# Where the two operands of a matmul start within a line of 256 bytes: MLP layers and output projection shifted by 128, 192 and 160 bytes

## The chip, the cores and the metric

The kernel runs on one core of one Trainium2 chip. The metric is the device time of one execution in microseconds. The kernel before was timed three times: 1135.06, 1134.04 and 1132.4 us, median 1134.04. A fourth execution was profiled and took 1130.94 us, with a span of 1129.1 us from its first to its last instruction.

## The reference

One layer of a streaming encoder on 512 frames of 1024 channels, all in float32. Three token mixers run on one input projection, their gated sum goes through an output projection, and a squared-ReLU MLP follows:

```
p   = rms_norm(x, g1) @ w_in                       # 1024 -> 11520 columns
m   = gate_a * y_a + gate_b * y_b + gate_c * y_c   # short conv, RG-LRU, RWKV-7
x   = x + m @ w_out                                # 1024 x 1024
h2  = rms_norm(x, g2)
x   = x + square(relu(h2 @ w1)) @ w2               # 1024 -> 4096 -> 1024
out = rms_norm(x, gf)
```

The mixers y_a, y_b and y_c matter here only as the work that runs before and beside the output projection.

## The kernel before

**Three matmuls for one product.** A float32 product is made of three matmuls in a reduced float32 format (`fp32r`). Each operand is split into a high part, a copy into that format, and a low part, the rest. `mm3` (L157 to L160) adds high × high, high × low and low × high in PSUM. In each matmul one operand is stationary: 128 × 128 values are loaded into TensorE by a separate instruction, the weight load ("PEld", LDWEIGHTS). The other is moving: 128 rows by 512 or 256 columns stream through. Every matmul has its own weight load, and the load for the next matmul runs while the present one streams.

**Weights of the network.** `load_half` (L132) fetches a 128 × 512 block on SP's queue, ACT copies it into `whi` (L136), and DVE subtracts to get `wlo` (L138, in the profile the helper's L99). Four buffers of each rotate. All blocks of `w_in`, `w_out`, `w1` and `w2` go this way, 340 half blocks in all.

**The stages that the change touches** come last:

- The output projection `w_out(th)` (L853) runs in two halves of 256 frames. For each of 8 output blocks and 8 input blocks it does one `mm3`: stationary a slice of `whi`/`wlo`, moving the merged `mh`/`ml` of `open_m` (L803). The first half is woven into the last part of the RWKV recurrence, the second runs alone. That is 2 × 8 × 8 × 3 = 384 matmuls of 256 columns, named `acc<-mh,whi` and the like in the profile. The result, scaled and split, is written into `h2h`/`h2l` (L862 to L864).
- The first MLP layer (`mlp1`, L908) does 32 blocks of 8 `mm3`, stationary `whi`/`wlo`, moving `h2h`/`h2l`, 512 columns each; the first block is done in two halves of 256. The squared ReLU is split into `ah`/`al` for the first 24 blocks and `ah2`/`al2` for the last 8 (L930 to L934).
- The second MLP layer (`mlp2`, L952) has the roles turned: stationary a 128-column slice of `ah`/`al` (or `ah2`/`al2`), moving `whi`/`wlo` with 512 columns. It keeps eight PSUM banks open and does 32 × 4 × 2 `mm3`.

**Places in memory.** Each tile has one start address, the same in all 128 partitions. `AL = 256` makes a tile start at a multiple of 256 bytes, `ALM = 2048` at a multiple of 2048. `whi`, `wlo`, `hh`, `hl` (the normalised input of the first projection), `mh`, `ml`, `ah2` and `al2` have AL; `h2h`, `h2l`, `ah` and `al` have ALM. A slice of 128 columns is 512 bytes and a row of 512 columns is 2048, so in all large matmuls before both operands start at 0 within a line of 256 bytes. A few small tiles of the mixers have no such demand. The program's memory plan puts them at other places within a line: `bd`, `bh` and `bl` at 128, `lgh`, `lgl`, `lws` and `las` at 224, `swah` and `swal` at 64, `swch`, `swcl`, `uh` and `ul` at 32. Their matmuls stand among those of the first projection (`pp<-hh,whi`).

The order of instructions is made when the program is built, by a planner with priorities; the change gives it the same instructions with the same shapes.

Of the kernel before, what the change touches and what calls it, by code (L numbers as in the profile page):

```python
# [10 lines left out]
F32R = mybir.dt.float32r  # L11
# [7 lines left out]
P = 128  # L19
# [10 lines left out]
S = 512  # L30

AL, ALM = 256, 2048
D = 1024
KT = 8
# [59 lines left out]
def block_kernel(ctx, tc, xt, win, par, mulr, sw, wout, w1, w2, fg, cst, eyes, out):  # L94
# [28 lines left out]
    x2d = dp.tile([4, P, D], F32, name="x2d")  # L123

    pv = lambda n, j: part[:, PI[n], j:j + 1]


    def load_w(src):
# [497 lines left out]
    def gate_c(pool, q, tag):  # L626
        gt = pool.tile([P, S], F32, tag=tag, name=tag, bufs=2 if tag[0] == "b" else 1)
        t = yield from proj(("gc", q))
        ac.activation(gt, t, AF.Tanh, bias=pv("mgc", q), scale=0.5)
        return gt  # L630

    def g2_mul(pool, q, gt):
        swh, swl = load_sw(pool, "swc", q, 4, 1)
        pg = pm.tile([P, S], F32, tag="pm", name="pg2")
        mm3(pg, swh[:, 0], swl[:, 0], lgh, lgl)
        stt(gt, gt, 1.0, pg, ADD, MUL)
# [13 lines left out]
    M = {"done": []}  # L650
# [112 lines left out]
    def fill_main(g):  # L763
        a = AB[g]
        if g + 1 == NG:
            yield from a
            return
        end = object()
        while not GS[g].inv_done:
            if next(a, end) is end:  # L770
                break
            yield
        while not GS[g].inv_done:
            yield
        b = krv(g + 1, GS[g + 1])
        live = [b, a]
        while live:
            for x_ in list(live):
                if next(x_, end) is end:
                    live.remove(x_)  # L780
                else:
                    yield
# [20 lines left out]
    def open_m():  # L803
        pk_ctx.close()
        mo = mo_ctx.enter_context(tc.tile_pool(name="mo", bufs=1))
        mh = M["mh"] = mo.tile([P, KT, S], F32R, name="mh", align_bytes=AL)
        ml = M["ml"] = mo.tile([P, KT, S], F32R, name="ml", align_bytes=AL)
        mab = M["mab"] = mo.tile([P, 2, S], F32, name="mab")
        for q in M["done"]:
            gp.dma_start(mh[:, q], mhd[q])  # L810
            gp.dma_start(ml[:, q], mld[q])
        gp.dma_start(mab, mpd[6:8].rearrange("q p t -> p q t"))
        M["mo"] = mo
        return
        yield

    def last_fill():
        yield from fill_main(NG - 1)
        M["gts"] = []
        for h in range(2):  # L820
            q = 6 + h
            gt = yield from gate_c(sp, q, f"bv{h}")
            g2_mul(wk, q, gt)
            M["gts"].append(gt)
            yield
        wk_ctx.close()
        ht_ctx.close()
        h2p = h2_ctx.enter_context(tc.tile_pool(name="h2p", bufs=1, side="right"))
        M["h2h"] = h2p.tile([P, KT, S], F32R, name="h2h", align_bytes=ALM)
        M["h2l"] = h2p.tile([P, KT, S], F32R, name="h2l", align_bytes=ALM)  # L830
        xrp = xr_ctx.enter_context(tc.tile_pool(name="xrp", bufs=1, side="right"))
        M["xrp"] = xrp
        x2T = M["x2T"] = xrp.tile([P, KT, S], F32, name="x2T")
        for i in range(4):
            gp.dma_start(x2T[:, 2 * i:2 * i + 2], xt[2 * i:2 * i + 2].rearrange("k p t -> p k t"))
        while "half" not in M:
            yield
        fin_m(0)
        yield from w_out(0)
# [3 lines left out]
    def fin_m(th):  # L843
        tl = slice(th * HT, (th + 1) * HT)
        for h in range(2):
            y = G_.v[h][:, tl]
            tt(y, y, G_.bv[h][:, tl], ADD)
            stt(y, y, 0.5, M["gts"][h][:, tl], MUL, MUL)
            tt(y, y, M["mab"][:, h, tl], ADD)
            ac.copy(M["mh"][:, 6 + h, tl], y)  # L850
            tt(M["ml"][:, 6 + h, tl], y, f(M["mh"][:, 6 + h, tl]), SUB)

    def w_out(th):  # L853
        tl = slice(th * HT, (th + 1) * HT)
        for mo in range(KT):
            w = load_w(wout[mo])
            acc = pp.tile([P, S], F32, tag="pp", name="acc")[:, 0:HT]
            for q in range(KT):
                mm3(acc, *wslice(w, q), M["mh"][:, q, tl], M["ml"][:, q, tl], start=q == 0, stop=q == KT - 1)
            x2 = M["x2T"][:, mo, tl]  # L860
            tt(x2, acc, x2, ADD)
            hi = M["h2h"][:, mo, tl]  # L862
            ac.activation(hi, x2, AF.Copy, scale=pv("n2", mo))
            stt(M["h2l"][:, mo, tl], x2, pv("n2", mo), f(hi), MUL, SUB)  # L864
            yield
# [15 lines left out]
    def post_half(th):  # L881
        yield from post_norm(NG - 1, G_, 4 * th, 4 * th + 4)
        if th == 0:
            M["half"] = True

    fl = last_fill()
    segments([(chainit(amat(G_), inverse(G_), open_m()), R4),
              (chainit(chain(G_, 0, 4), post_half(0), chain(G_, 4, NC), post_half(1)), R5)], fl)
    drain(fl)
# [3 lines left out]
    h2h, h2l = M["h2h"], M["h2l"]  # L893
# [6 lines left out]
    NA = 3 * NF // 4  # L900
    with tc.tile_pool(name="mw", bufs=2) as mw, \
            tc.tile_pool(name="ap", bufs=1) as apool, \
            ExitStack() as apool2:
        ahs = [apool.tile([P, NA, S], F32R, name="ah", align_bytes=ALM)]
        als = [apool.tile([P, NA, S], F32R, name="al", align_bytes=ALM)]
        ahl = lambda fi: (ahs[fi // NA][:, fi % NA], als[fi // NA][:, fi % NA])

        def mlp1(t, w, tl):  # L908
# [5 lines left out]
        for fi in range(NF):  # L914
            t = pp.tile([P, S], F32, tag="pp", name="p1")
# [150 lines left out]
```

## Time and profile before

| What | Value |
|---|---|
| Median of three runs | 1134.04 us |
| Profiled execution, its own time | 1130.94 us |
| Its span | 1129.1 us |
| TensorE busy (PE) | 1090.0 us, 97% |
| Weight loads busy (PEld) | 866.7 us, 77% |
| VectorE (DVE) and ScalarE (ACT) busy | 786.8 and 549.2 us |
| Mean granted TensorE clock | 0.984 |
| Output projection, first and last matmul | 709.0 to 768.7 us |
| First MLP layer, first and last matmul | 768.8 to 945.0 us |

A matmul's busy time runs from its start to its modelled end and overlaps that of the next one, since matmuls are pipelined; what a stream costs is the distance between the starts. Rows of groups show line, engine, operation, output and inputs, the stationary part's size, the moving part's size and type, the count, the busy time in us and the mean of one in ns, then the idle time before them. For three stretches of time the profile also lists each engine's busy time and count, then the granted clock, the share of DMA and its GB/s.

### The profile page before, as it was taken

How to read it: one execution, taken by the hardware profiler on the slowest of the kernel's cores; microseconds unless marked ns; L12 is line 12 of the kernel's file. 1: busy time of each engine (PE TensorE's matmuls, PEld its weight loads, DVE VectorE, ACT ScalarE, POOL GpSimd, SP SyncE). 2: the span in 40 equal slices, each digit the busy share in tenths (PEclk: the TensorE clock that was granted, in tenths of full speed). 3: DMA queues.
4: the chain of work that ended last, by engine and by line, in shares of the span. 5: the costliest groups of instructions: out<-in, count | busy, mean ns of one | idle time of the engine just before them, and what ended most of it. 6: DMA issues, size and time to landing. Idle time of an engine off the chain costs nothing.

```text
span 1129.1 us, 17256 instructions
## 1 busy us (share of the span) xinstructions
PE 1090.0 (97%) x6396; PEld 866.7 (77%) x6396; DVE 786.8 (70%) x1537; ACT 549.2 (49%) x1005; POOL 59.6 (5%) x99
## 2 busy tenths in 40 slices
PE   8899989999989999989999989999999999999996
PEld 4677867678777778777778767899888888888885
DVE  7998996889986989986888967686544544222225
ACT  6655356544466634466644465565444443222224
POOL 3200000000000000000000020100000000000003
PEclk8899988999999999999999999999999999999999
DMA  5222222222233222233222262555323225322232
GB/s 183 80 98 66 84 78 73 65 91 71 89 104 103 67 89 71 89 108 93 66 94 69 75 191 99 170 181 167 100 93 103 94 95 187 101 93 93 97 106 88
DMA packets 61973, 114.69 MB, mean 102 GB/s; under 512 B 7232, under 2 KB 10816, under 8 KB 61888
## 3 DMA queue, kind: packets, MB, share of 16 engines
q1 hardware_dynamic: 54960, 95.49, 25.7%
q0 software_dynamic: 6352, 17.30, 4.8%
q8 instruction: 50, 0.82, 0.3%
q10 hardware_dynamic: 576, 0.79, 0.2%
q14 instruction: 35, 0.29, 0.1%
HBM read 104.64 MB, written 8.91 MB: 101 GB/s over the span
## 4 chain that ended last, share of the span: by engine, by line
PE 82%; DVE 13%; issue 3%; ACT 2%; DMA 0%; SPq 0%; DVEq 0%; ACTq 0%
PE pp L160 12%; PE pp L158 12%; PE pp L159 11%; PE acc L159 6%; PE acc L158 6%; PE acc L160 6%; PE p L160 5%; PE p L159 5%; PE p L158 5%; DVE wlo L99 3%; PE pA L463 2%; DVE Z L99 2%; DVE dg L99 2%; PE py L570 1%; PE pu L555 1%
## 5 line engine op out<-in xcount | busy, mean ns | idle before, releaser
L99 DVE TENSOR_TENSOR wlo<-raw,whi 128x512 fp32r<-128x512 f32 x340 | 235.7, 696 | 231.4 <-ACT whi L136 222.7
L136 ACT CAST whi<-raw 128x512 fp32r<-128x512 f32 x340 | 209.6, 619 | 353.4 <-PE acc L160 123.1
L160 PE MATMUL pp<-hh,wlo 128*128 128x512 f32 x696 | 280.8, 404 | 18.5 <-DVE wlo L99 18.4
L159 PE MATMUL pp<-hl,whi 128*128 128x512 f32 x696 | 277.8, 399 | 3.1 <-DVE hl L102 3.1
L158 PE MATMUL pp<-hh,whi 128*128 128x512 f32 x696 | 278.5, 402 | 1.6 <-ACT hh L259 1.5
L160 PEld LDWEIGHTS pp<-hh,wlo 128*128 128x128 f32 x696 | 132.1, 190 | 55.4 <-DVE wlo L99 27.9
L159 PEld LDWEIGHTS pp<-hl,whi 128*128 128x128 f32 x696 | 132.2, 190 | 31.0 <-DVE hl L102 3.7
L158 PEld LDWEIGHTS pp<-hh,whi 128*128 128x128 f32 x696 | 132.2, 190 | 29.9 <-ACT hh L259 1.9
L160 PE MATMUL p<-h2h,wlo 128*128 128x512 f32 (+1 forms) x264 | 101.2, 383 | 0.0
L158 PE MATMUL p<-h2h,whi 128*128 128x512 f32 (+1 forms) x264 | 101.2, 383 | 0.0
L159 PE MATMUL p<-h2l,whi 128*128 128x512 f32 (+1 forms) x264 | 101.0, 383 | 0.0
L159 PE MATMUL acc<-wlo,ah 128*128 128x512 f32 x256 | 99.7, 389 | 0.0
L158 PE MATMUL acc<-whi,ah 128*128 128x512 f32 x256 | 99.6, 389 | 0.0
L160 PE MATMUL acc<-whi,al 128*128 128x512 f32 x256 | 99.6, 389 | 0.0
L159 PEld LDWEIGHTS p<-h2l,whi 128*128 128x128 f32 x264 | 49.6, 188 | 9.7
L158 PEld LDWEIGHTS p<-h2h,whi 128*128 128x128 f32 x264 | 49.6, 188 | 9.6
L160 PEld LDWEIGHTS p<-h2h,wlo 128*128 128x128 f32 x264 | 49.6, 188 | 9.5
L159 PEld LDWEIGHTS acc<-wlo,ah 128*128 128x128 f32 x256 | 48.0, 188 | 10.1 <-DVE wlo L99 0.3
L158 PEld LDWEIGHTS acc<-whi,ah 128*128 128x128 f32 x256 | 48.0, 188 | 10.1
L160 PEld LDWEIGHTS acc<-whi,al 128*128 128x128 f32 x256 | 48.0, 188 | 10.0
L99 DVE TENSOR_TENSOR Z<-Z,dg 64x31 f32<-64x31 f32 (+15 forms) x124 | 42.2, 340 | 4.1
L99 DVE TENSOR_TENSOR dg<-Z 64x31 f32<-64x31 f32 (+15 forms) x124 | 42.2, 340 | 4.1
(299 smaller groups left out, 1532.3 us busy)
## 6 DMA issues: line engine op xcount, KB each, us to landing
raw<-in_win SPq DMA_DIRECT2D x180, 256.0 KB, 2.6
raw<-in_w SPq DMA_DIRECT2D x128, 256.0 KB, 2.6
raw<-in_wout SPq DMA_DIRECT2D x32, 256.0 KB, 2.6
swr<-in_sw SPq DMA_DIRECT2D x16, 128.0 KB, 2.2
x2T<-in_xt POOLq DMA_DIRECT2D x4, 512.0 KB, 6.2
x2d<-st POOLq DMA_DIRECT2D x8, 256.0 KB, 2.9
xr<-x2d POOLq DMA_DIRECT2D x1, 2048.0 KB, 9.1
xT<-in_xt SPq DMA_DIRECT2D x3, 512.0 KB, 6.4
```

The costliest lines, as they stand in the source:

```text
L99: return v.tensor_tensor(out=o, in0=a, in1=b, op=op)
L136: ac.copy(hi, raw)
L158: pe.matmul(ps, wh, xh, start=start, stop=False)
L159: pe.matmul(ps, wh, xl, start=False, stop=False)
L160: pe.matmul(ps, wl, xh, start=False, stop=stop)
L463: pe.matmul(pts[h][:, ci], G_.BK[rows, jj, c], G_.AR[rows, jj, c], start=True, stop=True)
L555: pin(e != 0, pe.matmul(pu[64 * h:64 * h + 64, jj], AXt[rows, e, c, 0], sv[rows, e], start=True, stop=True))
L570: mm = pe.matmul(py[64 * h:64 * h + 64, jj], w, x, start=first and jj == 0, stop=last, skip_group_check=True)
```

## The change

Six tiles get a new start within the line of 256 bytes. A helper makes a tile that is longer by some bytes, on a multiple of 256, and returns the part behind them, seen as blocks of 512 columns:

```diff
+    def shifted(pool, n, name, by):
+
+        t = pool.tile([P, by // 4 + n * S], F32R, name=name, align_bytes=AL)
+        return t[:, by // 4:].rearrange("p (k t) -> p k t", k=n)
...
-        mh = M["mh"] = mo.tile([P, KT, S], F32R, name="mh", align_bytes=AL)
-        ml = M["ml"] = mo.tile([P, KT, S], F32R, name="ml", align_bytes=AL)
+        mh = M["mh"] = shifted(mo, KT, "mh", 160)
+        ml = M["ml"] = shifted(mo, KT, "ml", 160)
...
-        M["h2h"] = h2p.tile([P, KT, S], F32R, name="h2h", align_bytes=ALM)
-        M["h2l"] = h2p.tile([P, KT, S], F32R, name="h2l", align_bytes=ALM)
+        M["h2h"] = shifted(h2p, KT, "h2h", 128)
+        M["h2l"] = shifted(h2p, KT, "h2l", 128)
...
-        ahs = [apool.tile([P, NA, S], F32R, name="ah", align_bytes=ALM)]
-        als = [apool.tile([P, NA, S], F32R, name="al", align_bytes=ALM)]
+        ahs = [shifted(apool, NA, "ah", 64)]
+        als = [shifted(apool, NA, "al", 64)]
```

`whi` and `wlo` stay at 0. Counted from the stationary to the moving operand, the difference is 160 in the output projection and 128 in the first layer, where the shifted tile moves, and 0 - 64 = 192 modulo 256 in the second layer, where it is stationary. `ah2`, `al2` and the first projection's `hh`, `hl` keep their places. The start of the six tiles changes from a multiple of 2048 (of 256 for `mh` and `ml`) to one of 256 plus the shift.

## The prediction

> **What bounds the kernel now.** I read the page first, for the engine that sets the end and for the stretches in which it has no gap.
>
> ```profile
> span 1129.1 us, 17256 instructions
> PE 1090.0 (97%) x6396; PEld 866.7 (77%) x6396; DVE 786.8 (70%) x1537; ACT 549.2 (49%) x1005; POOL 59.6 (5%) x99
> PEclk8899988999999999999999999999999999999999
> PE 82%; DVE 13%; issue 3%; ACT 2%; DMA 0%; SPq 0%; DVEq 0%; ACTq 0%
> ```
>
> TensorE is busy for 97% of the span and carries 82% of the chain that ended last. Next the busy time in three stretches: the first MLP layer, the second, and the output projection.
>
> ```profile
> 773.70:944.70 171.00, 171.00 (x768) 141.75 (x767) 86.70 (x132) 76.20 (x133) 2.17 (x4) 1.00 0.31 103
> 945.30:1105.00 159.70, 159.70 (x706) 132.26 (x705) 41.86 (x61) 37.80 (x61) 1.29 (x2) 1.00 0.33 112
> 709.00:773.50 64.50, 63.66 (x600) 59.81 (x599) 50.57 (x119) 38.49 (x86) 5.11 (x8) 1.00 0.55 180
> ```
>
> In both layers PE has no idle time at the full clock, and DVE and ACT are busy for about half of the time or less. In the projection PE is idle for 0.84 of 64.5 us. So here the time is the number of matmuls times the distance from one start to the next, and a nanosecond on each moves the end by as much. The groups of the whole run count them:
>
> ```profile
> L158 PE MATMUL p<-h2h,whi 128*128 128x512 f32 x248 | 96.7, 390 | 0.0
> L158 PE MATMUL p<-h2h,whi 128*128 128x256 f32 x16 | 4.5, 283 | 0.0
> L158 PE MATMUL acc<-whi,ah 128*128 128x512 f32 x256 | 99.6, 389 | 0.0
> L159 PE MATMUL acc<-ml,whi 128*128 128x256 f32 x128 | 37.0, 291 | 0.0
> ```
>
> Each product has three such groups: 744 matmuls of 512 columns and 48 of 256 in the first layer, 768 of 512 in the second, 384 of 256 in the projection. The timeline of TensorE gives the distance. Its columns are start and duration in us; between the two rows of a pair lie 196, then 136 steps.
>
> ```profile
> 799.73 0.39 PE L158 MATMUL p<-h2h,whi 128*128 128x512 f32 x1
> ...
> 844.15 0.39 PE L159 MATMUL p<-h2l,whi 128*128 128x512 f32 x1
> ...
> 752.27 0.28 PE L158 MATMUL acc<-mh,whi 128*128 128x256 f32 x1
> ...
> 768.59 0.28 PE L159 MATMUL acc<-ml,whi 128*128 128x256 f32 x1
> ```
>
> 44.42 us / 196 = 226.6 ns and 16.32 us / 136 = 120.0 ns. 256 columns more cost 106.6 ns, that is 0.4166 ns a column, so 512 columns are 213.3 ns, and each matmul pays about 13.3 ns beyond its columns, whatever its length. At half the clock it doesn't:
>
> ```profile
> 34.50:36.70 2.20, 2.20 (x7) 1.73 (x6) 2.20 (x5) 0.72 (x1) 0.00 (x0) 0.50 0.00 0
> ```
>
> ```profile
> 34.51 0.63 PE L160 MATMUL pp<-hh,wlo 128*128 128x512 f32 x1
> ...
> 36.64 0.63 PE L160 MATMUL pp<-xgh,wlo 128*128 128x512 f32 x1
> ```
>
> With the granted clock at 0.50, five steps take 2.13 us, 426 ns each: 512 columns at twice 0.4166 and nothing more. The loss thus doesn't stretch with the array's clock; I take it (inferred) for a loss in feeding the operands. Feeding is doubled here, because every matmul runs beside the weight load of the next, which starts with it:
>
> ```profile
> 900.14 0.39 PE L160 MATMUL p<-h2h,wlo 128*128 128x512 f32 x1
> 900.14 0.19 PEld L158 LDWEIGHTS p<-h2h,whi 128*128 128x128 f32 x1
> ```
>
> **The change, part by part.** No instruction is added, removed or moved. The moving rows of a matmul now start 128 bytes (first layer) or 160 bytes (projection) past the place of the next weights in a line of 256, and 192 in the second layer, for the 24 of 32 blocks in `ah` and `al`: 24 × 24 = 576 matmuls. Before, all these differences are 0. The last 8 blocks (`ah2`, `al2`) keep 0.
>
> What a difference does is seen only where the earlier stages mix tiles. There I use the duration, which the group view gives in whole ns: in an even stream it is 389, and when the next matmul comes late it grows by nearly as much. These rows are windows cut to single matmuls, by difference between a matmul's moving operand and the next weights. First 0, and 128 (`hh` at 0, then `bd` at 128), at 410.5 us:
>
> ```profile
> L159 PE MATMUL pp<-hl,whi 128*128 128x512 f32 x1 | 0.4, 389 | 0.0
> L160 PE MATMUL pp<-hh,wlo 128*128 128x512 f32 x1 | 0.4, 396 | 0.0
> ```
>
> 128 the other way round (`bl` at 128, then `whi` at 0), at 94.9 us:
>
> ```profile
> L450 PE MATMUL pb<-bl,bd 128*128 128x512 f32 x1 | 0.4, 392 | 0.0
> ```
>
> 192 (`lgh`, `lgl` at 224, then `swc` at 32), at 701.7, 701.9 and 246.6 us:
>
> ```profile
> L158 PE MATMUL pg<-lgh,swch 128*128 128x512 f32 x1 | 0.4, 393 | 0.0
> L159 PE MATMUL pg<-lgl,swch 128*128 128x512 f32 x1 | 0.4, 398 | 0.0
> L159 PE MATMUL pg<-lgl,swch 128*128 128x512 f32 x1 | 0.4, 392 | 0.0
> ```
>
> 160 (`lws`, `las` at 224, then `swa` at 64), two neighbours at 534.3 us and two at 363.8:
>
> ```profile
> L408 PE MATMUL pw<-lws,swal 128*128 128x512 f32 x1 | 0.4, 397 | 0.0
> L413 PE MATMUL pa<-las,swah 128*128 128x512 f32 x1 | 0.4, 398 | 0.0
> ...
> L408 PE MATMUL pw<-lws,swal 128*128 128x512 f32 x1 | 0.4, 392 | 0.0
> L413 PE MATMUL pa<-las,swah 128*128 128x512 f32 x1 | 0.4, 394 | 0.0
> ```
>
> All lie 3 to 9 ns above 389, and of two neighbours with the same difference the second isn't nearer to 389 than the first. The same excess stands at difference 0 for some matmuls after a stall, so 389 is a state into which a stream settles; none of these rows has 512 columns and a settled stream at another difference. That is the gap in the evidence.
>
> First layer: (7 + 3) / 2 = 5 ns × 744 = +3.7 us; bounds 3 × 744 and 7 × 744, 2.2 to 5.2. Second: (4 + 9 + 3) / 3 = 5.3 ns × 576 = +3.1 us; bounds 1.7 to 5.2. PE has no gap in either that could cover this.
>
> The projection has 256 columns. A stream of 256 that isn't settled yet stands at the start of the first layer:
>
> ```profile
> 769.26 0.28 PE L158 MATMUL p<-h2h,whi 128*128 128x256 f32 x1
> ...
> 769.85 0.28 PE L160 MATMUL p<-h2h,wlo 128*128 128x256 f32 x1
> ```
>
> Five steps in 0.59 us, 118 ns: faster than the settled 120. The weight loads of the settled stream bear it out (min/median/max in ns; the second row is mostly 512 columns):
>
> ```profile
> L158 PEld LDWEIGHTS acc<-mh,whi x128: 186/192/193, 708.8 to 768.4; 128*128 128x128 f32 x128
> L158 PEld LDWEIGHTS p<-h2h,whi x264: 187/188/192, 768.7 to 944.3; 128*128 128x128 f32 x132
> ```
>
> At 256 columns the load takes 192 against 188, so there settling costs both operands something. For the projection's 384 and the first layer's 48 I take -2 ns: -0.9 us. Upper bound, from the row with the difference 160 though with 512 columns: +9 × 384 = +3.5 us.
>
> The writes into the shifted tiles cost nothing more: a copy or a subtraction into a tile off the line (`uh` at 32) takes what it takes on it (`ah`):
>
> ```profile
> L153 ACT CAST uh<-u 128x512 fp32r<-128x512 f32 x8 | 5.0, 621 | 25.9 <-DVE u L102 25.9
> L933 ACT CAST ah<-r 128x512 fp32r<-128x512 f32 x32 | 19.9, 621 | 26.7 <-DVE r L99 26.7
> L99 DVE TENSOR_TENSOR ul<-u,uh 128x512 fp32r<-128x512 f32 x8 | 5.5, 692 | 0.5
> L99 DVE TENSOR_TENSOR al<-r,ah 128x512 fp32r<-128x512 f32 x32 | 22.2, 693 | 22.0 <-ACT ah L933 22.0
> ```
>
> Were one dearer by 100 ns, DVE's and ACT's idle half in the first layer would cover it. The loads of `mh` and `ml` from memory start by 672 us, 37 us ahead of the projection:
>
> ```profile
> L810 POOL DMA_DIRECT2D mh<-mhd x5: 536/566/597, 667.8 to 672.0; - x5
> ```
>
> Sum: 3.7 + 3.1 - 0.9 = **+5.9 us**. On the profiled execution's own 1130.94 us (span 1129.1) that is 1136.8; the median of the runs, 1134.04, lies 3.1 higher, and the predicted time is the median's, **1140**.
>
> **The rivals.** *The pairs lose less than now: faster.* If the 13.3 ns are collisions of the two reads in one place of the line, parting them should remove some. For it: the loss is missing at half clock, and durations follow the addresses. Against it: every row above. The price: removed altogether, 13.3 × (744 + 576 + 48 + 384) = -23.3 us, 1110.7; with 2 ns off each, -3.5 us, 1130.5. It decides as soon as a settled stream at the new difference has its starts under 226 ns apart.
>
> *The stream settles all the same: no change.* Load and matmul start together at any difference, and over 128 columns the load passes two lines of 256 whichever place it starts from, so the time may slip until 389 returns. Price 0: 1134. The Trainium skill, "TensorE: Matmul & The Clock Gate", section Step-by-step, says that TensorE reads moving operand and weights through two independent ports, so that a load takes nothing from a running matmul; by that rule the places couldn't matter at all. The 389 to 398 ns speak against it, as they change with the tiles' places. The same page's Back-to-back issue gap gives about 216 ns for 512 columns at the full clock; the estimate by that figure, 10.9 ns less on each of the 1752, would be -19 us.
>
> *It doesn't settle and collides throughout: much slower.* All at +9: 9 × (744 + 576 + 384) = +15.3 us, 1149.4. It belongs to the forecast's sign, as its upper end.
>
> *The change does something else.* A flat tile seen through a view could be tracked more coarsely, so that the first layer's first half waits for the last columns of `h2h`. That is one copy of the row below and one subtraction, about +1 us; I give it no chance of its own.
>
> ```profile
> L863 ACT ACTIVATE h2h<-x2T,part 128x256 fp32r<-128x256 f32 x16 | 8.1, 508 | 1.0 <-DVE x2T L99 1.0
> ```
>
> **How the numbers follow.** Slower as forecast, both sizes: 0.50. No change: 0.16. Faster: 0.34, half of it by more than 8 us. No change means within 0.2%, 2.3 us, about what a measurement of this kernel can tell. If it is slower, from +1.7 us to +15.3: 1136 to 1149. For 8 times in 10 the range must reach into the faster case, to 1117, leaving out its deepest part.
>
> **What would show it.** Right: an even stream with starts 230 to 233 ns apart and durations of 392 to 396 in the first layer and in three quarters of the second, 226.6 back at `ah2`, and 117 to 119 in the projection. Each layer can go its own way, since each has its own difference. Wrong: 226.6 everywhere, or any stage below it; and if the stages keep their distances while the time moves, the cause lies elsewhere.

## The result and the profile after

The changed kernel took 1140.61 us, median of three runs (1139.85 to 1143.39), against 1134.04 before: a ratio of 1.0074, 95% interval 1.0055 to 1.0093, or 6.2 to 10.5 us. The forecast was 1140. The profiled execution is the median one, with a span of 1138.8 us. Ratios here and below are of fast runs; one execution of 2721.66 us, with all differences back to 0, counts as slow and is left out of its ratio. The page has the same instructions and nearly the same division of the chain of waits:

```profile
span 1138.8 us, 17256 instructions
PE 1099.7 (97%) x6396; PEld 867.5 (76%) x6396; DVE 786.6 (69%) x1537; ACT 548.7 (48%) x1005; POOL 58.5 (5%) x99
PE 81%; DVE 14%; issue 3%; ACT 2%; DMA 0%; SPq 0%; DVEq 0%; ACTq 0%
```

PE's busy time grew by 9.7 us, as much as the span; DVE, ACT and the weight loads have what they had. The stretches of time show where, in the order projection, first layer, second layer and with the same windows as before:

```profile
709.00:773.50 64.50, 63.63 (x600) 59.43 (x599) 49.81 (x118) 39.16 (x86) 5.09 (x8) 1.00 0.54 181
773.70:944.70 171.00, 171.00 (x751) 138.05 (x750) 84.55 (x130) 74.10 (x129) 2.16 (x4) 1.00 0.31 102
945.30:1105.00 159.70, 159.70 (x689) 129.08 (x688) 42.05 (x61) 37.63 (x61) 1.29 (x2) 1.00 0.33 111
```

In 171 us of the first layer 751 matmuls start instead of 768, in 159.7 us of the second 689 instead of 706, with PE still without a gap at the full clock. The projection's window has 600, as before. The timeline of TensorE gives the distances, by the first and the last row of a stretch; the stages stand in the order first layer (172 steps), second layer with `ah` (172), second layer with `ah2` (111), projection (131):

```profile
799.83 0.39 PE L163 MATMUL p<-h2h,whi 128*128 128x512 f32 x1
...
839.96 0.39 PE L164 MATMUL p<-h2l,whi 128*128 128x512 f32 x1
...
959.65 0.39 PE L164 MATMUL acc<-wlo,ah 128*128 128x512 f32 x1
...
999.78 0.39 PE L165 MATMUL acc<-whi,al 128*128 128x512 f32 x1
...
1089.74 0.39 PE L164 MATMUL acc<-wlo,ah 128*128 128x512 f32 x1
...
1114.90 0.39 PE L164 MATMUL acc<-wlo,ah 128*128 128x512 f32 x1
...
753.81 0.28 PE L164 MATMUL acc<-ml,whi 128*128 128x256 f32 x1
...
769.36 0.28 PE L163 MATMUL acc<-mh,whi 128*128 128x256 f32 x1
```

The second layer of the kernel before, over 177 steps:

```profile
999.65 0.39 PE L158 MATMUL acc<-whi,ah 128*128 128x512 f32 x1
...
1039.77 0.39 PE L158 MATMUL acc<-whi,ah 128*128 128x512 f32 x1
```

40.13 / 172 = 233.3 ns in the first layer and in the shifted part of the second, 25.16 / 111 = 226.7 in its unshifted last quarter, 15.55 / 131 = 118.7 in the projection. Against 226.6, 40.12 / 177 = 226.7 and 120.0 before, that makes 6.7 × 744 = +5.0 us, 6.6 × 576 = +3.8 and -1.3 × 384 = -0.5, together +8.3 us, inside the interval. The weight loads in the projection fell back to 188 ns, the change from 192 that the prediction read from them:

```profile
L163 PEld LDWEIGHTS acc<-mh,whi x128: 186/188/194, 710.2 to 769.2; 128*128 128x128 f32 x128
L163 PE MATMUL acc<-mh,whi x128: 277/280/387, 710.4 to 769.4; 128*128 128x256 f32 x128
```

The projection's first matmul came at 710.4 us instead of 709.0. Nothing ahead of it was changed, and in the four other kernels below, which leave what runs ahead of it alone too, it starts between 709.4 and 712.6, so I don't count these 1.4 us to the change. With the 8.3 us of the stages they make up the 9.7 us between the two spans.

### The profile page after: what moved, and what is told of

Same layout as the page of the kernel before. It is cut to its first block, busy times and chain, and to the rows that moved or that the text cites. A ratio compares the mean times of both kernels' runs of the same rounds, so it can differ in the third digit from the quotient of the medians.

```text
span 1138.8 us, 17256 instructions
## 1 busy us (share of the span) xinstructions
PE 1099.7 (97%) x6396; PEld 867.5 (76%) x6396; DVE 786.6 (69%) x1537; ACT 548.7 (48%) x1005; POOL 58.5 (5%) x99
## 4 chain that ended last, share of the span: by engine, by line
PE 81%; DVE 14%; issue 3%; ACT 2%; DMA 0%; SPq 0%; DVEq 0%; ACTq 0%
PE pp L165 11%; PE pp L163 11%; PE pp L164 11%; PE acc L164 6%; PE acc L165 6%; PE acc L163 6%; PE p L165 5%; PE p L164 5%; PE p L163 5%; DVE wlo L99 3%; PE pA L468 2%; DVE Z L99 2%; DVE dg L99 2%; PE py L575 1%; PE pu L560 1%
```

## The experiments

Theory A is the prediction's: the difference between a matmul's moving operand and the next weights, within a line of 256 bytes, decides. "The table" is the first experiment. Ratios are to the kernel before, timed again beside the experiments: median 1131.15 us of 19 runs for the first two kernels below, 1133.69 us of 17 for the last two. Each of the three programs of bare streams ran once, with a mean granted clock of 1.0.

**A table of streams.** A program of its own runs 120 equal matmuls for each difference, with eight weight slices and four moving rows in turn:

```diff
+        for i in range(N):
+            k = (i % 8) if step else 0
+            pe.matmul(ps[0:m, 0:cols], b[:, k * P:k * P + m], a[:, k // 2, 0:cols],
+                      start=i == 0, stop=i == N - 1)
```

> This program leaves the encoder out: it only runs streams of 120 equal matmuls, each with its own weight load, and gives out sums of their results. Within a stream the moving operand starts a fixed number of bytes past the place of the weights in a line of 256, and the streams go through 0, 16, 32 ... 240 for 512 and for 256 columns, then 256, 512 and 1024, then both operands moved together by 32, 128 and 192, then weights of 64 and of 32 columns, then a stream that uses the same addresses for all its matmuls. Theory A (the difference within the line decides, through collisions of the two reads): 226.7 ns from start to start at 0, 256, 512, 1024 and in the three streams with both operands moved; about 233 at 128 and 192; the others somewhere from 227 to 237. With 64 and 32 weight columns the part beyond the 213.3 ns of the columns (13.3 at difference 0) falls with the load, to about 7 and 3. Rival B (a moving row that starts off the line costs, whatever the weights do): the three streams with both moved are as slow as those with the same shift alone, over 230. Rival C (the loss is a fixed one for changing weights): 13.3 ns stay with 64 and 32 weight columns.

The distance from start to start, mean over the last 89 steps of each stream, in ns:

| Difference | 512 columns | 256 columns | | Difference | 512 columns | 256 columns |
|---|---|---|---|---|---|---|
| 0 | 226.7 | 120.0 | | 128 | 232.3 | 118.7 |
| 16 | 231.6 | 118.7 | | 144 | 233.3 | 118.7 |
| 32 | 233.3 | 116.7 | | 160 | 234.3 | 117.4 |
| 48 | 233.4 | 118.4 | | 176 | 233.3 | 119.3 |
| 64 | 228.9 | 117.8 | | 192 | 233.4 | 113.3 |
| 80 | 231.1 | 120.0 | | 208 | 234.7 | 119.2 |
| 96 | 233.3 | 120.0 | | 224 | 233.4 | 118.3 |
| 112 | 231.2 | 113.3 | | 240 | 226.7 | 117.2 |

The timeline merges a stream into one row: start, length, count. The distance is the length less one matmul's duration (0.39 us, 0.28 for 256 columns), over the count less one. In this order: 512 columns at 0, 64, 128 and 192; 256 columns at 0, 112 and 192; both operands moved by 128; 32 weight columns at 0.

```profile
19.63 22.63 PE L77 MATMUL c_d<-mv,wt 128*128 128x512 f32 x99
...
133.68 20.30 PE L77 MATMUL c_d<-mv,wt 128*128 128x512 f32 x88
...
244.73 20.61 PE L77 MATMUL c_d<-mv,wt 128*128 128x512 f32 x88
...
356.72 20.46 PE L77 MATMUL c_d<-mv,wt 128*128 128x512 f32 x87
...
464.78 10.48 PE L77 MATMUL c_d<-mv,wt 128*128 128x256 f32 x86
...
564.24 10.02 PE L77 MATMUL c_d<-mv,wt 128*128 128x256 f32 x87
...
635.74 9.00 PE L77 MATMUL c_d<-mv,wt 128*128 128x256 f32 x78
...
805.69 17.62 PE L77 MATMUL both<-mv,wt 128*128 128x512 f32 x77
...
881.68 23.56 PE L77 MATMUL w_d<-mv,wt 128*32 128x512 f32 x101
```

Worked out: 226.9, 228.9, 232.4, 233.4; 120.0, 113.3, 113.2; 226.7; 231.7 (the first row still holds a few steps before the stream settled). For 512 columns no difference beats 0. For 256 columns 0 is among the worst, and 112 and 192 are 6.7 ns better. With both operands moved by 32, 128 or 192 the stream stays at 226.7, which rules rival B out: a moving row off the line costs nothing by itself. Differences of 256, 512 and 1024 give 226.7 too. One expectation of Theory A fell: with 64 and 32 weight columns the loss didn't shrink with the load but rose, to 230.0 and 231.7 ns. Rival C's constant 226.7 fell with it. The stream that uses the same addresses for all its matmuls took 226.7 ns at 0 and 232.4 at 128, so the effect doesn't need changing addresses.

**All differences back to 0, the rest of the change kept.**

```diff
-        mh = M["mh"] = shifted(mo, KT, "mh", 160)
+        mh = M["mh"] = shifted(mo, KT, "mh", 256)
...
-        M["h2h"] = shifted(h2p, KT, "h2h", 128)
+        M["h2h"] = shifted(h2p, KT, "h2h", 256)
...
-        ahs = [shifted(apool, NA, "ah", 64)]
+        ahs = [shifted(apool, NA, "ah", 256)]
```

(The same for `ml`, `h2l` and `als`.)

> The changed kernel with all shifts set to 256 bytes: the tiles are flat and seen through a view, and start at a multiple of 256 instead of 2048, but every difference within the line is 0 again. Theory A (the difference decides): time as before, within 0.3% of 1134 us, and starts 226.7 ns apart in both layers and 120 in the projection. Rival D (the flat tiles, the lost multiple of 2048 or another plan of the memory cost the time): about 1140 us, as with the change.

The ratio to the kernel before was 1.0018, 0.9998 to 1.0037. The first layer's timeline, 177 steps:

```profile
799.82 0.39 PE L163 MATMUL p<-h2h,whi 128*128 128x512 f32 x1
...
839.93 0.39 PE L163 MATMUL p<-h2h,whi 128*128 128x512 f32 x1
```

40.11 / 177 = 226.6 ns; the second layer has 226.7 too. The flat tiles, their view and the lost multiple of 2048 cost nothing in the streams; rival D is out for them, and for the whole kernel no cost is resolved.

**The first layer alone.** From the changed kernel:

```diff
-        mh = M["mh"] = shifted(mo, KT, "mh", 160)
+        mh = M["mh"] = mo.tile([P, KT, S], F32R, name="mh", align_bytes=AL)
...
-        ahs = [shifted(apool, NA, "ah", 64)]
+        ahs = [apool.tile([P, NA, S], F32R, name="ah", align_bytes=ALM)]
```

> Only the first layer's moving operand shifted, by 128 bytes; the projection and the second layer as before. Theory A: the first layer's 741 distances of 512 columns sum to about 173.1 us instead of 168.3, as in the changed kernel, the second layer stays at 226.7 ns a matmul, and the kernel loses about 4.9 us, 1.0043 of the time before. Rival D (the plan of the memory as a whole): the loss doesn't divide by stages, and the first layer's distances differ from those of the changed kernel.

1.0040, 1.0021 to 1.0060: 4.5 us of 1131. First layer (172 steps), then second (177):

```profile
799.72 0.40 PE L164 MATMUL p<-h2l,whi 128*128 128x512 f32 x1
...
839.85 0.40 PE L165 MATMUL p<-h2h,wlo 128*128 128x512 f32 x1
...
999.67 0.39 PE L163 MATMUL acc<-whi,ah 128*128 128x512 f32 x1
...
1039.79 0.39 PE L163 MATMUL acc<-whi,ah 128*128 128x512 f32 x1
```

233.3 and 226.7 ns: the loss divides by stages, and each stage's is that of its own difference.

**The projection alone, at 192.**

```diff
-        mh = M["mh"] = mo.tile([P, KT, S], F32R, name="mh", align_bytes=AL)
-        ml = M["ml"] = mo.tile([P, KT, S], F32R, name="ml", align_bytes=AL)
+        mh = M["mh"] = shifted(mo, KT, "mh", 192)
+        ml = M["ml"] = shifted(mo, KT, "ml", 192)
```

> Only the projection's moving operand shifted, by 192 bytes; both layers as before. By the table of streams (113.3 ns a matmul of 256 columns at the difference 192, 120.0 at 0) Theory A expects the projection's even stretches at 113 and, over 384 matmuls less those after a pause, 1.5 to 2.5 us less: about 0.998 of the time before, at the edge of what can be measured, with 226.7 ns in both layers. Rival E (the streams of the table don't carry over to a kernel in which the weights come from rotating buffers): 116 to 120 ns and no gain.

0.9997, 0.9979 to 1.0014. In the second half of the projection (131 steps):

```profile
753.81 0.28 PE L165 MATMUL acc<-mh,wlo 128*128 128x256 f32 x1
...
768.96 0.28 PE L164 MATMUL acc<-ml,whi 128*128 128x256 f32 x1
```

15.15 / 131 = 115.6 ns, against 120.0. Most single distances are 113 or 114, so the table carries over to rotating buffers. Two distances in this stretch, 295 and 223 ns, are no part of the even stream; without them it is 113.4. At the first a weight load waited for DVE, which had not finished the next `wlo` (the last bracket is the idle time before and what ended it):

```profile
760.79 0.19 PEld L165 LDWEIGHTS acc<-mh,wlo 128*128 128x128 f32 x1 [0.21 <-DVE wlo L99]
```

The gain by these rows, 4.4 × 384 = 1.7 us or 0.15%, is within the interval and not shown in the time.

**Other differences that the table calls good.** From the changed kernel, 160 becomes 112, 128 becomes 240, and `ah`, `al` move from 64 to 16, so that the second layer has 0 - 16 = 240:

```diff
-        mh = M["mh"] = shifted(mo, KT, "mh", 160)
+        mh = M["mh"] = shifted(mo, KT, "mh", 112)
...
-        M["h2h"] = shifted(h2p, KT, "h2h", 128)
+        M["h2h"] = shifted(h2p, KT, "h2h", 240)
...
-        ahs = [shifted(apool, NA, "ah", 64)]
+        ahs = [shifted(apool, NA, "ah", 16)]
```

> All six tiles stay shifted, but by other amounts: 112 in the projection, 240 in the first layer, and 16 in the second, where the difference is 0 - 16 = 240. By the table of streams Theory A expects 113.3 ns in the projection and 226.7 in both layers, although no difference is 0: a time 0 to 2.5 us below before. A rival by which any difference but 0 costs expects 230 ns and more in the layers and about 1140 us.

1.0089, 1.0067 to 1.0112: no better than the change itself (the intervals overlap), and not what Theory A expected from the table. First layer (170 steps), second layer (172), projection (127):

```profile
799.72 0.40 PE L163 MATMUL p<-h2h,whi 128*128 128x512 f32 x1
...
839.95 0.40 PE L165 MATMUL p<-h2h,wlo 128*128 128x512 f32 x1
...
979.68 0.40 PE L163 MATMUL acc<-whi,ah 128*128 128x512 f32 x1
...
1019.81 0.40 PE L164 MATMUL acc<-wlo,ah 128*128 128x512 f32 x1
...
753.84 0.28 PE L164 MATMUL acc<-ml,whi 128*128 128x256 f32 x1
...
768.40 0.28 PE L165 MATMUL acc<-mh,wlo 128*128 128x256 f32 x1
```

236.6, 233.3 and 114.6 ns. At 240 the table's 226.7 didn't return, and the rival's 230 ns and more stood in both layers; at 112 the projection got nearly all of its 113.3.

**Other lengths, half the bytes, finer steps.** The table's program with other streams, among them operands in bfloat16:

```diff
+    for c in (448, 384, 320, 128):
+        for r in (0, 64, 112, 192, 240):
+            g.append((f"c{c}_d{r}", c, r, 0, 128, F32R))
...
+    for c in (512, 256):
+        for r in (0, 128):
+            g.append((f"half{c}_d{r}", c, r, 0, 128, BF16))
```

> The encoder is left out again; streams of 120 matmuls, now with 448, 384, 320 and 128 columns at the differences 0, 64, 112, 192 and 240, with 64 weight columns at four differences, in bfloat16 (half the bytes on both sides) with 512 and 256 columns, and in steps of 4 bytes around the best differences. The table showed 226.67 ns for 512 columns at best and 113.33 for 256, both 17/16 of the columns' own 213.33 and 106.67. Theory F (moving operands of 4 bytes lose one part in 16 whatever the weights do, and collisions come on top): at the best difference 198.3 ns for 448 columns, 170.0 for 384 and 141.7 for 320. Rival G (a fixed 13.3 ns for each change of weights): 200.0, 173.3 and 146.7 at best. In bfloat16 F expects at most half the loss or none (213 to 220 ns for 512 columns), and a smaller effect of the difference; G expects 226.7. In steps of 4 bytes a sharp optimum would show at one step; a wide one of 16 bytes or more would be the same for its neighbours.

Merged rows again, a duration being 0.36, 0.33, 0.31, then 0.38 us: the best of 448, 384 and 320 columns (at 64, 0 and 0), then 512 columns in bfloat16 at 0 and at 128.

```profile
386.74 15.96 PE L70 MATMUL c_d<-mv,wt 128*128 128x448 f32 x79
...
482.79 14.37 PE L70 MATMUL c_d<-mv,wt 128*128 128x384 f32 x82
...
585.75 12.92 PE L70 MATMUL c_d<-mv,wt 128*128 128x320 f32 x87
...
854.64 17.65 PE L70 MATMUL half_d<-mv,wt 128*128 128x512 bf16 x81
...
880.76 17.43 PE L70 MATMUL half_d<-mv,wt 128*128 128x512 bf16 x80
```

200.0, 173.3 and 146.6 ns are G's numbers, the columns and a fixed 13.3; F, one part in 16, is out. But G's fixed loss isn't a rule either, as 256 columns reach 113.3, a loss of 6.7. Nor is 0 always the best place: 448 columns take 202.7 ns there. With 320 columns the five differences gave the same 146.7 ns, and with 128 the same 111.7, where the columns alone are 128 × 0.4166 = 53.3. In bfloat16 the distance is 215.9 and 215.8: a loss of 2.5 ns, where G expected 226.7, and no effect of the difference between 0 and 128. The finer steps break the table's smoothness: for 256 columns 108 and 116 give 120.0 and 121.7 around the 113.3 at 112, and for 512 columns 4 bytes give 236.6.

**Several states at one difference.** A third program repeats streams with other neighbours, after a rest, with weights 256 bytes further on, and in the kernel's pattern of three:

```diff
+        if kind == "plain":
+            return col(wa, i), row(hi[d], i % 8 // 2)
+        if kind == "far":
+            return col(wb, i), row(hi[d], i % 8 // 2)
+        if kind == "mix":
+            k, j = i // 3, i % 3
+            return col(wa if j == 2 else wb, k), row(lo[d] if j == 1 else hi[d], k)
```

> The encoder is left out; streams of 120 matmuls that ask why the difference 240 gave 226.7 ns in the table and 236.7 in the kernel. Theory H (the difference alone doesn't fix the distance: where it isn't 0 a stream can settle in more than one state): at 240 the repeated streams, those after a rest of TensorE and those with the kernel's pattern of three give distances from 226 to 237 that differ by more than 3 ns among themselves, while at 0 all give 226.7. Rival I (the places beyond the line count, as the kernel's high and low weights lie 256 bytes apart): the repeats agree with one another within 1 ns, and weights 256 bytes further on or the pattern of three change the distance at 240. Two more streams tell which load collides: weights and moving operands at 0 and 128 in turn, so that each matmul's difference to its own weights is 0 and to the next ones 128, and the other way round. Theory A (the load that runs beside a matmul is that of the next one): about 232 where the next differs by 128, 226.7 where the next differs by 0. If the matmul's own weights counted, it would be the reverse.

The program has four plain streams at 240. Three of them, merged (a duration is 0.40 us), then the two streams with alternating places, 64 and 88 steps:

```profile
181.70 17.68 PE L85 MATMUL plain_d<-h,wa 128*128 128x512 f32 x74
...
264.62 18.60 PE L85 MATMUL again_d<-h,wa 128*128 128x512 f32 x79
...
319.77 19.57 PE L85 MATMUL again_d<-h,wa 128*128 128x512 f32 x82
...
852.65 0.40 PE L85 MATMUL own0next<-h,wc 128*128 128x512 f32 x1
...
867.80 0.40 PE L85 MATMUL own0next<-h,wc 128*128 128x512 f32 x1
...
875.65 0.39 PE L85 MATMUL own128next<-h,wc 128*128 128x512 f32 x1
...
895.89 0.39 PE L85 MATMUL own128next<-h,wc 128*128 128x512 f32 x1
```

At 240: 236.7, 233.3 and 236.7 (the fourth, too, has 236.7), and 226.7 in the table: three states at one difference, which is Theory H. At 128 two plain streams took 232.3 and 233.4. Rival I is out: weights 256 bytes further on and the pattern of three gave the plain stream's distance to 0.1 ns at every difference tried. At 0 all five streams gave 226.7 (the repeat, the rest and the pattern among them); at 112 and 192 with 256 columns all four gave 113.3. Alternating places give 236.7 where the next weights differ and 230.0 where the matmul's own do. Theory A expected about 232 and 226.7, the reverse if the own weights counted, and neither came out: both loads seem to count. Which counts for more isn't shown, as each stream ran once and 236.7 is more than the 232.3 of a plain stream at 128, where both weights differ.

## Why the prediction was right, point by point

*What bounds the kernel.* Right: in both layers a longer distance between starts went to the end undiminished, with PE at no idle time before and after. The signs that the prediction named came out too: 233.3 ns against 230 to 233 in both layers, 226.7 back at `ah2`, 118.7 in the projection.

*The first layer*, 5 ns × 744 = +3.7 us: the sign and the cause (the difference of the two places) held, the size was low. Measured 6.7 ns, +5.0 us. *The second layer*, 5.3 ns × 576 = +3.1: measured 6.6 ns, +3.8. Both terms were means over single pairs of the earlier stages. A whole stream at such a difference sits at the upper half of what those pairs showed (3 to 9 ns), and the two layers, at 128 and 192, come out alike. The gap that the prediction named, whether a stream settles at another difference, is closed in a way that it didn't list: it settles into a repeating pattern, but a slower one.

*The projection*, -2 ns on 384 and 48 matmuls, -0.9 us: measured -1.3 on the 384, -0.5 us. The sign was right, but the reading behind it, that loads of 192 ns instead of 188 mark the loss, was luck. At the differences 0 (table) and 184 (other lengths) a stream of 256 columns runs at 120.0 ns alike, with different loads:

```profile
L77 PEld LDWEIGHTS c_d<-mv,wt 128*128 128x128 f32 x76 | 9.2, 192 | 0.0
...
L70 PEld LDWEIGHTS c_d<-mv,wt 128*128 128x128 f32 x93 | 11.2, 188 | 0.0
```

The first layer's 48 showed no change worth counting.

*The sum* of +5.9 us against +8.3 by the stages and +6.6 between the medians. That 1140 was met to 0.6 us is partly luck: the medians moved by less than the stages add up to.

*The loss as a loss in feeding the operands.* Only half carried. The 13.3 ns don't belong to the array's columns (they are absent at half the clock, and the same for 320, 384, 448 and 512 columns at their best difference), but "whatever its length" was too wide: 256 columns can pay 6.7, and 128 columns pay 58.3. They go with `fp32r`, since bfloat16 pays 2.5; whether through the bytes or the format isn't separated. That the weight load causes them is not shown: a load of a quarter of the columns left a longer distance at the difference 0, not a shorter one, and no stream ran without loads.

*The rivals.* "Faster" was false at 512 columns for every difference tried, at least in the states met, and true at 256 and, at 64, for 448. "The stream settles all the same" was false at 128, 160 and 192 with 512 columns, true for one stream at 240, and true for 320 columns at every difference tried. The rule of the Trainium skill ("TensorE: Matmul & The Clock Gate", section Step-by-step) that a load takes nothing from a running matmul agrees with the bfloat16 streams, the same at 0 and at 128. For 4-byte operands the distances of 226.7 to 236.7 at one length and one clock differ from it, and the measurement decides. The 216 ns of that page's Back-to-back issue gap, which the section gives for a single isolated matmul, is met by streams of bfloat16 (215.9) and by no stream of 4-byte operands with 512 columns.

*What stays open.* That the time follows the difference, though not by it alone, is shown; why is not: whether two accesses collide and which, why 256 columns have better places than 0 and 320 columns don't care, and what chooses among the states at 240. The two alternating streams don't settle which weights' place counts.

## What to carry to other kernels

Where matmuls of 4-byte operands run back to back, measure the distance between their starts, not their busy time: PE was 100% busy at 226.7 and at 233.3 ns. Give both operands of a 512-column `fp32r` stream the same place within a line of 256 bytes; it was the one choice that always settled into the best distance met here. With 256 columns try 112 and 192, and check any such place in the kernel itself: with the projection at 192 one weight load had to wait for DVE's `wlo`.

## What the runs showed of the hardware beyond the expected

- At one difference a stream of equal matmuls can run in several steady states: 226.7, 233.3 and 236.7 ns at 240.
- The best difference depends on the length: at 0, 512 columns have their best distance and 256 columns 6.7 ns more than theirs. With 320 columns it makes no difference (146.7 ns at all five).
- A step of 4 bytes can decide: 113.3 ns at 112, 120.0 at 108.
- Narrower weights don't help at the difference 0 (226.7 ns with 128 weight columns, 230.0 with 64 and 231.7 with 32) and little at 128 (232.3, 231.1 and 230.7).
